# Four token blocks through the dense expert pass instead of three, with both expert tables split in two

## The chip, the cores and the metric

The kernel runs on one core of a Trainium2 chip. The metric is the device time of one execution in microseconds (us). Three runs of the kernel before gave a median of 3335.54 us (3333.65 to 3341.8).

## The reference

One decoder layer over 1024 tokens of width 1024, in float32. A token mixer (stick-breaking attention and an mLSTM) and a layer norm give `h`; what follows is a feed-forward layer of 16384 experts ("PEER"), of which each token uses 8 heads x 16:

```
s1, s2 = scores of h against two sets of 128 keys        # per head
idx, gates = top 16 of the 256 sums of the two top-16s   # expert = 128*i1 + i2
act = gelu(h . u_tab[idx])                               # 128 rows of 1024 per token
out = sum over the 128 chosen of gates * act * v_tab[idx]
h   = LN(alpha*h + out + sigmoid(h Wg) * (p Wp))
```

## The kernel before

Tokens are cut into 8 blocks of 128, which pass through the mixer in three groups, (0, 1), (2, 3, 4) and (5, 6, 7) (`BLOCKS`). Below, blocks are called by these numbers, 0 to 7. Per group `main()` issues: projections, then attention and mLSTM, then `branch` (gates, output projection, layer norm), `keys` (key scores and the top 16 of each half, on VectorE), then `choose` (top 16 of the sums, softmax; one block after the other, ending in the tile `vidx` of expert numbers) merged with `embed` (the `p Wp` part, tile `gs`) and the next group's projections.

The expert layer is done in two ways.

**Gathered** blocks (0, 1, 2, 5, 6): `Experts.first` fetches for each of the block's 128 choices one row of `u` per token by an indirect DMA on the GpSimd queue (line 1079, tile `vr`, six buffers) and VectorE multiplies and sums it (line 1099); `Experts.second` does the same with `v` (line 1111). Both are recorded by the helper in line 139. One such instruction with its DMA is called a row below: 256 rows a block, 512 KB each. A rate table places the rows between the other work, so each engine's order is fixed when the program is built; a layer norm ends each block.

**Dense** blocks (3, 4, 7, `DENSE`): `spread` (line 954) writes each block's gates as a matrix over all 16384 experts to DRAM (`Gd`): one-hot columns by VectorE and ScalarE (`ohA`, `ohB`, lines 977 to 985; the letters in `HOTS` say which engine does each of four), a product on TensorE (line 987), copies (line 989) and stores. `dense` (line 1009) then takes the experts in 128 steps of 128. A step loads 512 KB of `u` and 512 KB of `v`, splits `u` into a high and a low part of a shorter format (`split`, line 249: ScalarE copies, VectorE subtracts), scores with three products (line 273) of 384 columns for each of 8 slices, takes Gelu, multiplies by the gates (line 1043) and, one step later (`back`, line 1016), adds `y` times the unsplit float32 `v` into six PSUM banks for three blocks. Float32 products run in two passes. At the end `based` is added and a layer norm is taken.

The group that goes last issues in this order: split the dense blocks' inputs (`halve`), `keys`, `choose` of block 7 merged with `embed`, then `choose` of 5 and 6 merged with `dense`.

Of the kernel before, what the change touches and what calls it, by code (L numbers as in the profile page):

```python
# [18 lines left out]
D = 1024  # L19
S = 1024  # L20
P = 128
# [44 lines left out]
BLOCKS = [(0, 1), (2, 3, 4), (5, 6, 7)]  # L66
DENSE = (3, 4, 7)
OFF = (0, 256, 0)
# [4 lines left out]
SLOTS = 5  # L73
W = 384
# [45 lines left out]
def body(ctx: ExitStack, tc: tile.TileContext, a, out):  # L120
# [62 lines left out]
    def c6(name, shape=(P, 4, W), dt=F32):  # L183
        return sb.tile(list(shape), dt, name=name, tag="c6", bufs=8)

    def c4(name, shape=(P, D)):
        return sb.tile(list(shape), F32, name=name, tag="c4", bufs=NC4)

# [5 lines left out]

    def csel(name, shape=(P, 512)):
        return sb.tile(list(shape), F32, name=name, tag="cs", bufs=NCS)

# [55 lines left out]
    def load_piece(ap):  # L253
        wf = T([P] + list(ap.shape[1:]), F32, "wf", 8)
        dma.dma_start(wf, ap)
        return wf

    def split_piece(wf):
        if wf.shape[1] == 2:
            hl = [T([P, 2, 512], F32R, "wf", 8) for _ in range(2)]  # L260
            split(wf, *hl)
            return hl
        halves = []
        for i in range(2):
            halves.append([c2("hl", (P, 4, P), F32R) for _ in range(2)])
            split(wf[:, 4 * i:4 * i + 4, :], *halves[i])
        return halves
# [61 lines left out]
    def load_ln(i):  # L329
        r = []  # L330
        for n in "gb":
            src = a[f"ln{i}_{n}"]
            t = T([P, D], F32, f"ln2{n}") if i == 2 else c4(f"ln{n}_")
# [79 lines left out]
    ND = len(DENSE)  # L413
    Gd = dr.tile([ND, 8, 2, P, 64, 16], F32, name="Gd")

# [62 lines left out]
    def project(o):  # L478
# [25 lines left out]
        o.qT = c6("qT")  # L504
        o.vx = T([P, 3, NM, 129], F32, "vx", 1)
        vec.memset(o.vx[:, :, :, 128:129], 1.0)
# [447 lines left out]
    def spread(tb, vidx, gt):  # L954
# [7 lines left out]
        vec.tensor_copy(f, ii)  # L962
        by = HOTS
        pt = PT("z", (P, 4, P))
# [7 lines left out]
        for q in range(8):  # L972
# [19 lines left out]
            for i in range(2):  # L992
                dma.dma_start(Gd[d, q, i], st[i])

    def slot(tb):
        o = [o for o in blks if tb in o.tbs][0]
        j = tb - o.tbs[0]
        return o.h1T[:, :, j * P:(j + 1) * P]

    def halve():  # L1000

        r = [[c6("h1s", dt=F32R) for _ in range(2)] for _ in range(2)]
        for q in range(2):
            for d, tb in enumerate(DENSE):
                c = slice(d * P, (d + 1) * P)
                split(slot(tb)[:, 4 * q:4 * q + 4, :], *[t[:, :, c] for t in r[q]])
        return r

    def dense(h1s):

        w = ND * P
        acc = [[PT("g"), PT("g")], [PT("g"), PT("g")], [PT("z"), PT("z")]]
        gp = [[c6("gp", (P, 4 * ND, 8, 16)) for _ in range(2)] for _ in range(2)]
        todo = []

        def back(e, y, wv):
            for d in range(ND):
                for c in range(2):
                    pe.matmul(acc[d][c], y[:, d * P:(d + 1) * P], wv[:, c * 512:(c + 1) * 512],  # L1019
                              start=e == 0, stop=e == P - 1)  # L1020

        def load(e):
            if e < P:
                i, k = divmod(e, 64)
                src = Gd[:, :, i, :, k:k + 8, :].rearrange("d q p i t -> p (d q) i t")
                for c in range(2):
                    dma.dma_start(gp[e // 8 % 2][c], src[:, 4 * ND * c:4 * ND * (c + 1)])

        load(0)
        for e in range(P):  # L1030
            if e % 8 == 0:
                load(e + 8)
            wu = stream.get(experts[e][0])
            wv = stream.get(experts[e][1])[0]
            pu = PT("m")
            for k in range(8):
                i, j = divmod(k, 4)
                mm(pu[:, :w], [t[:, j, :] for t in wu[i]], [t[:, j, :] for t in h1s[i]], k == 0, k == 7)
            y = csel("y")[:, :w]
            act.activation(y, pu[:, :w], AF.Gelu)  # L1040
            y3 = y.rearrange("p (c a t) -> p c a t", c=2, t=16)
            for c in range(2):
                vec.tensor_tensor(y3[:, c], y3[:, c], gp[e // 8 % 2][c][:, :, e % 8, :], op=OP.mult)  # L1043
            todo.append((e, y, wv))
            if len(todo) > 1:
                back(*todo.pop(0))
            yield 9.2
        back(*todo.pop(0))
        g, b = ln2
        hs = []  # L1050
        for d, tb in enumerate(DENSE):
            h = c4("accd")
            dma.dma_start(h, based[tb * P:(tb + 1) * P, :])
            for c in range(2):
                cs = slice(c * 512, (c + 1) * 512)
                vec.tensor_tensor(h[:, cs], h[:, cs], acc[d][c], op=OP.add)
            hs.append(h)
        for d in layer_norm(hs, g, b):
            dma.dma_start(out[DENSE[d] * P:(DENSE[d] + 1) * P, :], hs[d])
            yield 1.0  # L1060


    class Experts:
# [41 lines left out]
        def second(self, tb, w, vidx, gt):  # L1105
            act.loose(w, w, AF.Gelu)
            vec.tensor_tensor(w, w, gt.rearrange("p h k -> p (h k)"), op=OP.mult)
            acc = r4("acc")
            dma.dma_start(acc, based[tb * P:(tb + 1) * P, :])
            for s in range(P):  # L1110
                self.row(vidx, s, (a["v"], lambda vr, s=s: evec.scalar_tensor_tensor(
                    acc, vr, w[:, s:s + 1], acc, op0=OP.mult, op1=OP.add)))
                yield ROW_US
            self.flush()
            g, b = ln2
# [22 lines left out]

    ln2 = []

    def main():
        yield from pre(blks[0])
        ln2.extend(load_ln(2))
        for i, o in enumerate(blks):
# [12 lines left out]
            else:  # L1157
                h1s = halve()
                yield from keys(o)
                ex.rate = RATES["last"]  # L1160
# [78 lines left out]
```

## Time and profile before

| what | value |
|---|---|
| median of three runs | 3335.54 us |
| the profiled execution, its own time | 3336.88 us |
| its span, first to last instruction | 3335.1 us |
| TensorE busy | 2974.0 us (89%) |
| VectorE busy | 2668.9 us (80%) |
| ScalarE busy | 1101.9 us (33%) |
| GpSimd busy | 1562.8 us (47%) |
| DMA, mean over the span | 310 GB/s |

Shares of busy time are averages over stages with different limits, so the stages are to be read one by one. Matmuls overlap in the records: the time that one costs is the distance from its start to the next start, and not its own length.

### The profile page before, as it was taken

The numbers are of one execution on the slowest core, as the hardware profiler recorded it, in microseconds if no ns is written. First come the engines' busy times: TensorE is split into PE (matmuls) and PEld (weight loads), VectorE is DVE, ScalarE is ACT, GpSimd is POOL, SyncE is SP. The second block draws the span as 40 slices with busy tenths as digits, with TensorE's granted clock in tenths as the row PEclk, the third lists the DMA queues.
The fourth block names the chain that finished last, engine by engine and source line by source line (L and its number), as shares of the span: only waits on it lengthen the run. The fifth ranks groups of instructions, "written<-read, shape, count | busy, mean of one in ns | idle before, by whom it ended". The sixth has DMA issues, their size and how long they took to land.

```text
span 3335.1 us, 38987 instructions
## 1 busy us (share of the span) xinstructions
PE 2974.0 (89%) x12105; PEld 1982.6 (59%) x12105; DVE 2668.9 (80%) x5661; ACT 1101.9 (33%) x2560; POOL 1562.8 (47%) x1313
## 2 busy tenths in 40 slices
PE   7997999969899837999898967899999999999990
PEld 6786654545464535556655545566666666666660
DVE  5635999788699999989887999967776777777788
ACT  4626234430611458556413145111111111111110
POOL 0000156557534553556665343644445555554565
PEclk9998998969999968999899989999999999999995
DMA  6444699989979989898799889999999999999997
GB/s 213 136 146 143 234 350 323 323 281 381 376 271 317 359 273 320 306 340 267 244 373 363 308 303 312 335 361 352 353 346 355 357 353 348 348 355 337 361 329 265
DMA packets 341825, 1035.22 MB, mean 310 GB/s; under 512 B 38512, under 2 KB 95216, under 8 KB 341616
## 3 DMA queue, kind: packets, MB, share of 16 engines
q0 software_dynamic: 184320, 671.17, 56.0%
q1 hardware_dynamic: 157296, 361.55, 30.3%
q8 instruction: 96, 1.57, 0.2%
q14 instruction: 113, 0.93, 0.1%
HBM read 991.17 MB, written 41.42 MB: 310 GB/s over the span
## 4 chain that ended last, share of the span: by engine, by line
PE 67%; DVE 16%; issue 8%; ACT 6%; DMA 2%; POOL 1%; SPq 0%; DVEq 0%; POOLq 0%; ACTq 0%
PE g L274 15%; PE g L1019 13%; PE z L1019 6%; PE m L278 5%; PE m L276 5%; PE m L277 5%; PE g L784 3%; DVE acc L139 3%; PE m L622 3%; ACT ohB L161 2%; PE z L583 2%; DVE vr L139 2%; PE g L276 2%; PE g L278 2%; PE g L277 2%
## 5 line engine op out<-in xcount | busy, mean ns | idle before, releaser
L1079 POOL DMA_INDIRECT vr<-in_u_dram,vidx x640 | 772.9, 1208 | 1013.1 <-DVE V L139 384.5
L1079 POOL DMA_INDIRECT vr<-in_v_dram,vidx x640 | 786.1, 1228 | 729.6 <-DVE acc L139 271.2
L139 DVE SCALAR_TENSOR_TENSOR acc<-vr,w,acc 128x1024 f32<-128x1024 f32 x640 | 817.9, 1278 | 43.6 <-DMA vr<-in_v_dram,vidx 34.4
L139 DVE SCALAR_TENSOR_TENSOR vr<-vr,h1r 128x1024 f32<-128x1024 f32 x640 | 780.0, 1219 | 55.8 <-DMA vr<-in_u_dram,vidx 40.9
L1019 PE MATMUL g<-wf,y 128*128 128x512 f32 x1024 | 462.8, 594 | 14.7 <-DVE y L1043 14.7
L161 ACT ACTIVATE hl<-wf 128x512 fp32r<-128x512 f32 x256 | 160.5, 628 | 765.7 <-PE m L278 599.5
L251 DVE TENSOR_TENSOR hl<-wf,hl 128x512 fp32r<-128x512 f32 x256 | 179.1, 701 | 292.8 <-PE m L277 244.7
L276 PE MATMUL m<-h1s,hl 128*128 128x384 f32 x1024 | 394.7, 385 | 3.5 <-ACT y L161 3.5
L278 PE MATMUL m<-h1s,hl 128*128 128x384 f32 x1024 | 347.8, 340 | 2.7 <-DVE hl L251 2.6
L274 PE MATMUL g<-hT,wf 128*128 128x384 f32 x1024 | 342.7, 489 | 5.8 <-DVE gs L851 3.2
L277 PE MATMUL m<-h1s,hl 128*128 128x384 f32 x1024 | 346.0, 338 | 0.0
L1019 PEld LDWEIGHTS g<-wf,y 128*128 128x128 f32 x1024 | 193.1, 190 | 201.9 <-issue 171.3
L274 PEld LDWEIGHTS g<-hT,wf 128*128 128x128 f32 x1024 | 191.7, 191 | 136.1 <-issue 7.7
L1019 PE MATMUL z<-wf,y 128*128 128x512 f32 x512 | 240.6, 592 | 0.0
L276 PEld LDWEIGHTS m<-h1s,hl 128*128 128x128 f32 x1024 | 194.1, 190 | 34.0 <-issue 29.4
L277 PEld LDWEIGHTS m<-h1s,hl 128*128 128x128 f32 x1024 | 194.1, 190 | 29.2 <-issue 29.2
L278 PEld LDWEIGHTS m<-h1s,hl 128*128 128x128 f32 x1024 | 193.8, 189 | 4.3 <-DVE hl L251 3.3
L987 PE MATMUL z<-ohA,ohB 128*128 128x128 f32 x768 | 137.9, 320 | 47.1 <-ACT ohB L161 18.7
L274 PE MATMUL g<-h1T,wf 128*128 128x384 f32 x512 | 173.1, 493 | 1.5 <-ACT h1T L161 1.4
L1019 PEld LDWEIGHTS z<-wf,y 128*128 128x128 f32 x512 | 97.3, 190 | 122.5 <-issue 122.2
L622 PE MATMUL m<-awT,vt 128*64 128x128 f32 x992 | 150.2, 303 | 18.6 <-ACT awT L173 10.4
L987 PEld LDWEIGHTS z<-ohA,ohB 128*128 128x128 f32 x768 | 112.1, 210 | 74.5 <-ACT ohB L161 53.1
(332 smaller groups left out, 4461.6 us busy)
## 6 DMA issues: line engine op xcount, KB each, us to landing
wf<-in_uE_dram SPq DMA_DIRECT2D x128, 512.0 KB
wf<-in_v_dram SPq DMA_DIRECT2D x128, 512.0 KB
wf<-in_wmain_dram SPq DMA_DIRECT2D x84, 512.0 KB
wf<-in_wgate_dram SPq DMA_DIRECT2D x48, 512.0 KB
wf<-in_wq_dram SPq DMA_DIRECT2D x48, 512.0 KB
Gd<-stage SPq DMA_DIRECT2D x48, 512.0 KB
gp<-Gd SPq DMA_DIRECT2D x32, 768.0 KB
wf<-in_wout_dram SPq DMA_DIRECT2D x24, 512.0 KB
```

Of the source, the lines that this page charges most:

```text
L139: x = getattr(vec, op)(*args, **kw)
L161: x = nc.scalar.activation(o, i, f, **kw)
L251: vec.tensor_tensor(lo, src, hi, op=OP.subtract)
L274: pe.matmul(o, l[0], r[0], start=first, stop=last)
L276: pe.matmul(o, l[0], r[0], start=first, stop=False)
L277: pe.matmul(o, l[0], r[1], start=False, stop=False)
L278: pe.matmul(o, l[1], r[0], start=False, stop=last)
L622: pe.matmul(po[rows, :P], vt[:, lo + s, row["e"] * 64:(row["e"] + 1) * 64], wT[:, s * P:(s + 1) * P], start=i == 0, stop=i == row["nb"] - 1)
L784: pe.matmul(acc, yT[k // 4][:, k % 4, n * P:(n + 1) * P], wo[u][k // 2][:, k % 2, :], start=k == 0, stop=k == 7)
L987: pe.matmul(pg[:, k], B[:, k], A[:, k], start=True, stop=True)
L1019: pe.matmul(acc[d][c], y[:, d * P:(d + 1) * P], wv[:, c * 512:(c + 1) * 512], start=e == 0, stop=e == P - 1)
L1079: pool.indirect_dma_start(out=vr, out_offset=None, in_=use[0], in_offset=bass.IndirectOffsetOnAxis(ap=idx[:, s:s + 1], axis=0))
```

## The change

Block 2 moves from the gathered blocks to the dense ones, so that 0, 1, 5 and 6 are gathered. In the dense pass `v` and `y` are split in two as `u` was, and the product with `v` becomes three products of the short format. Eight PSUM banks hold the sums of three blocks; the fourth block's product is taken for two steps at a time into a bank of the scoring pair (`pair`) and added up by VectorE in SBUF, in the place of block 5's `h1T`. `choose` of block 5 is issued ahead of the dense pass. `HOTS` for block 7 gives VectorE three of four one-hot columns. Gates are loaded for 6 steps at a time instead of 8. Pools change in size, and the last layer norm's vectors are loaded where they are used.

```
-DENSE = (3, 4, 7)
+DENSE = (7, 2, 3, 4)
+LAST = (5, 7)
+GE = 6
+NWF = 10
-HOTS = "DAAD"
+HOTS = {2: "DAAD", 3: "DAAD", 4: "DAAD", 7: "DDAD"}
...
     def split_piece(wf):
-        if wf.shape[1] == 2:
-            hl = [T([P, 2, 512], F32R, "wf", 8) for _ in range(2)]
+        if wf.shape[1] != 8:
+            hl = [T(list(wf.shape), F32R, "wf", NWF) for _ in range(2)]
...
-    stream.items += [(x, i == 0) for e in experts for i, x in enumerate(e)]
+    for e in range(P + 1):
+        stream.items += [(experts[e][0], True)] if e < P else []
+        stream.items += [(experts[e - 1][1], True)] if e else []
...
+        def score(e):
             wu = stream.get(experts[e][0])
-            wv = stream.get(experts[e][1])[0]
             pu = PT("m")
             for k in range(8):
                 i, j = divmod(k, 4)
-                mm(pu[:, :w], [t[:, j, :] for t in wu[i]], [t[:, j, :] for t in h1s[i]], k == 0, k == 7)
-            y = csel("y")[:, :w]
-            act.activation(y, pu[:, :w], AF.Gelu)
+                mm(pu, [t[:, j, :] for t in wu[i]], h1s[0][k], k == 0, k == 7)
+            y = csel("y")
+            act.activation(y, pu, AF.Gelu)
             y3 = y.rearrange("p (c a t) -> p c a t", c=2, t=16)
...
+            hl = c4("yhl", (P, 2, W4), F32R)
+            split(y, hl[:, 0], hl[:, 1])
+            ys[e] = hl
+
+        def part(o, e, d, c, first, last):
+            mm(o, [ys[e][:, i, d * P:(d + 1) * P] for i in range(2)],
+               [t[:, c * 512:(c + 1) * 512] for t in vs[e]], first, last)
+
+        def back(e):
+            vs[e] = stream.get(experts[e][1])
+            for d in range(n):
+                for c in range(2):
+                    part(acc[d][c], e, d, c, e == 0, e == P - 1)
+
+        def pair(e, c):
+            pg = PT("m")
+            part(pg, e, n, c, True, False)
+            part(pg, e + 1, n, c, False, True)
...
+                vec.tensor_tensor(s4, s4, p4, op=OP.add)
...
+        for e in range(P + 2):
+            if e % GE == 0:
+                load(e // GE + 1)
+            if e < P:
+                score(e)
+            if e % 2 and e > 1:
+                pair(e - 3, 1)
+            if 0 < e <= P:
+                back(e - 1)
+            if e % 2 == 0 and e:
+                pair(e - 2, 0)
...
-                yield from Merge(choose(o, [t for t in o.tbs if t in DENSE]), embed(o))
+                yield from Merge(choose(o, LAST), embed(o))
+                halve(h1s, [t for t in DENSE if t in o.tbs])
                 ex.rate = RATES["dense"]
-                yield from Merge(choose(o, [t for t in o.tbs if t not in DENSE]), dense(h1s))
+                yield from Merge(choose(o, [t for t in o.tbs if t not in LAST]), dense(h1s))
...
-    nc = bacc.Bacc("TRN2", target_bir_lowering=False, num_devices=1, dynamic_dma_scratch_size=8192)
+    nc = bacc.Bacc("TRN2", target_bir_lowering=False, num_devices=1, dynamic_dma_scratch_size=2048)
```

Three places show how the change moves instructions. Line numbers of the changed program stand a few higher (139 becomes 143, 276 to 278 become 280 to 282).

TensorE before, the end of a dense step: the last of 24 scoring products, the six float32 products of `back`, and the next step's scoring.

```order
L278 MATMUL m<-h1s,hl 128x384
L1019 MATMUL g<-wf,y 128x512 x4
L1019 MATMUL z<-wf,y 128x512 x2
L276 MATMUL m<-h1s,hl 128x384
L277 MATMUL m<-h1s,hl 128x384
```

TensorE now, the end of a scoring (`h1l` is the last low part of the inputs), two products of `back`, then the first three of a `pair`.

```order
L281 MATMUL m<-h1l,hl 128x512
L282 MATMUL m<-h1s,hl 128x512
L280 MATMUL g<-wf,yhl 128x512
L281 MATMUL g<-wf,yhl 128x512
L280 MATMUL m<-wf,yhl 128x512
L281 MATMUL m<-wf,yhl 128x512
L282 MATMUL m<-wf,yhl 128x512
```

A step has 24 scoring products of 512 columns, and 18 in `back` and on average 6 in `pair` (768 in all), in place of 24 of 384 columns and 6 in float32.

VectorE before, where block 2's `vidx` is ready: block 3's choice goes on behind it (`top`, `pos` and `cv` are its tiles).

```order
L139 SCALAR_TENSOR_TENSOR acc<-vr,w,acc 128x1024
L139 CAST vidx<-idf 128x128
L139 MAX top<-cv 128x8
L139 MAX_INDEX pos<-top,cv 128x8
```

VectorE now, at the same place.

```order
L143 CAST vidx<-idf 128x128
L143 SCALAR_TENSOR_TENSOR vr,w<-vr,h1r 128x1024
L966 TENSOR_SCALAR seli<-vidx 128x128
L967 TENSOR_SCALAR seli<-vidx 128x128
L143 SCALAR_TENSOR_TENSOR acc<-vr,w,acc 128x1024
L968 CAST self<-seli 128x256
```

Block 2's spread now stands between its `vidx` and the rest of block 3's choice, with rows of the gathered blocks among it.

VectorE before, in `keys` of the last group (`sc` holds scores, `V` and `I` the best values and places).

```order
L804 MAX V<-sc 128x8 x3
L807 MAX V<-sc 128x8 x3
L139 SCALAR_TENSOR_TENSOR acc<-vr,w,acc 128x1024
L805 MAX_INDEX I<-V,sc 128x8 x3
L808 MAX_INDEX I<-V,sc 128x8 x3
```

VectorE now, the same place.

```order
L810 MAX V<-sc 128x8 x3
L811 MAX_INDEX I<-V,sc 128x8 x3
L812 MATCH_REPLACE sc<-V,sc 128x128 x3
L813 MAX V<-sc 128x8 x3
L814 MAX_INDEX I<-V,sc 128x8 x3
```

No row stands in `keys` any more. Counted over VectorE's order, 736 rows stood ahead of the first dense gate product and 544 behind it; now 535 and 489.

## Rows read from the trace of the kernel before

**Rows 1.** The page, part 1: busy time by engine.
```profile
PE 2974.0 (89%) x12105; PEld 1982.6 (59%) x12105; DVE 2668.9 (80%) x5661; ACT 1101.9 (33%) x2560; POOL 1562.8 (47%) x1313
```

**Rows 2.** Busy time by stage: stretch, us, five engines, granted clock, DMA share, GB/s.
```profile
1015.00:1300.00 285.00, 206.45 (x860) 136.07 (x858) 277.22 (x762) 145.46 (x418) 134.75 (x108) 0.88 0.89 313
1300.00:1791.00 491.00, 448.72 (x1844) 274.00 (x1843) 420.45 (x637) 238.91 (x532) 293.33 (x239) 0.92 0.88 316
1791.00:1914.00 123.00, 123.00 (x432) 73.48 (x431) 116.87 (x413) 17.58 (x38) 51.20 (x52) 0.99 0.88 314
1914.00:2058.00 144.00, 105.53 (x468) 77.06 (x467) 139.77 (x405) 80.75 (x222) 54.73 (x49) 0.88 0.90 306
2058.00:3242.00 1184.00, 1166.13 (x4472) 802.05 (x4473) 873.93 (x1434) 206.60 (x376) 623.92 (x491) 0.99 0.96 348
```

**Rows 3.** TensorE in order of time, one dense step: start, length, line, operation.
```profile
2604.15 3.59 PE L1019 MATMUL g<-wf,y 128*128 128x512 f32 x8
...
2609.65 0.33 PE L278 MATMUL m<-h1s,hl 128*128 128x384 f32 x1
...
2613.29 0.34 PE L278 MATMUL m<-h1s,hl 128*128 128x384 f32 x1
2613.47 3.59 PE L1019 MATMUL g<-wf,y 128*128 128x512 f32 x8
```

**Rows 4.** TensorE in order of time, group one: ten split products of 512 columns.
```profile
131.21 0.39 PE L277 MATMUL g<-wf,vr 128*128 128x512 f32 x1
...
133.50 0.62 PE L276 MATMUL g<-wf,vr 128*128 128x512 f32 x2
```

**Rows 5.** VectorE instructions by line and form: busy us, mean ns, idle before.
```profile
L139 DVE SCALAR_TENSOR_TENSOR acc<-vr,w,acc 128x1024 f32<-128x1024 f32 x640 | 817.9, 1278 | 43.6 <-DMA vr<-in_v_dram,vidx 34.4 <-DMA acc<-based 1.1 <-DVE vr L139 0.9
L139 DVE SCALAR_TENSOR_TENSOR vr<-vr,h1r 128x1024 f32<-128x1024 f32 x640 | 780.0, 1219 | 55.8 <-DMA vr<-in_u_dram,vidx 40.9 <-issue 5.8 <-DVE vr L139 0.8
L251 DVE TENSOR_TENSOR hl<-wf,hl 128x512 fp32r<-128x512 f32 x256 | 179.1, 701 | 292.8 <-PE m L277 244.7 <-issue 39.8 <-PE m L278 4.1
L251 DVE TENSOR_TENSOR wf<-wf 128x1024 fp32r<-128x1024 f32 x68 | 83.0, 1221 | 73.9 <-ACT wf L161 71.8 <-PE g L784 2.1
L1043 DVE TENSOR_TENSOR y<-y,gp 128x192 f32<-128x192 f32 x256 | 80.4, 351 | 4.3 <-DMA gp<-Gd 4.3
L977 DVE TENSOR_TENSOR ohA<-iota,sel 128x512 f32<-128x512 f32 x96 | 65.4, 681 | 0.0
L985 DVE TENSOR_SCALAR ohB<-iota,sel 128x128 f32<-128x128 f32 x192 | 57.5, 339 | 0.0
```

**Rows 6.** VectorE in order of time: `vidx` of blocks 2, 3, 4 and 7.
```profile
1069.44 0.23 DVE L139 CAST vidx<-idf 128x128 uint32<-128x128 f32 x1
...
1105.61 0.21 DVE L139 CAST vidx<-idf 128x128 uint32<-128x128 f32 x1
...
1234.76 0.21 DVE L139 CAST vidx<-idf 128x128 uint32<-128x128 f32 x1
...
1972.04 0.22 DVE L139 CAST vidx<-idf 128x128 uint32<-128x128 f32 x1
```

**Rows 7.** TensorE's waits at 1015 to 1300 us (first row) and 1300 to 1791 us.
```profile
PE z L965 <- DVE rs L376: 40.4, 1, 40.4
...
PE m L394 <- ACT mx L161: 10.1, 1, 10.1
PE m L622 <- ACT awT L173: 6.7, 5, 2.9
```

**Rows 8.** The end, in order of time: TensorE's last products, and VectorE behind them.
```profile
3246.04 1.88 PE L1019 MATMUL z<-wf,y 128*128 128x512 f32 x4
...
3249.56 1.28 DVE L1056 TENSOR_TENSOR accd<-accd,z 128x512 f32<-128x512 f32 x2
3250.76 10.52 DVE L139 SCALAR_TENSOR_TENSOR acc<-vr,w,acc 128x1024 f32<-128x1024 f32 x8
...
3312.76 1.29 DVE L370 BATCH_NORM_STATS2 st<-acc 128x6 f32<-128x512 f32 x2
```

More of the change, by code (lines that the diff above doesn't have):

```diff
@@ L72 @@
 FASTQ = {0}
-SLOTS = 5
+SLOTS = 6
 W = 384
@@ L193, in c2, with csel @@
         return sb.tile(list(shape), dt, name=name, tag="c2", bufs=NC2)
-    def csel(name, shape=(P, 512)):
-        return sb.tile(list(shape), F32, name=name, tag="cs", bufs=NCS)
+    def csel(name, shape=(P, 512), dt=F32):
+        return sb.tile(list(shape), dt, name=name, tag="cs", bufs=NCS)
     first = [c4("xt") for _ in BLOCKS[0]]
@@ L253, in load_piece @@
     def load_piece(ap):
-        wf = T([P] + list(ap.shape[1:]), F32, "wf", 8)
+        wf = T([P] + list(ap.shape[1:]), F32, "wf", NWF)
         dma.dma_start(wf, ap)
@@ L332, in load_ln @@
             src = a[f"ln{i}_{n}"]
-            t = T([P, D], F32, f"ln2{n}") if i == 2 else c4(f"ln{n}_")
+            t = T([P, D], F32, "vr", K) if i == 2 else c4(f"ln{n}_")
             dma.dma_start(t, bass.AP(tensor=src.tensor, offset=src.offset, ap=[[0, P], [1, D]]))
@@ L992, in spread @@
             for i in range(2):
[L993 to L1007, printed above, removed]
+                dma.dma_start(Gd[d, q, :, i * 64:(i + 1) * 64], st[i])
@@ new lines, in body, with halve, parts @@
+    W4 = ND * P
+    def halve(h1s, tbs):
+        for tb in tbs:
+            c = slice(DENSE.index(tb) * P, (DENSE.index(tb) + 1) * P)
+            for k, n, hi, lo in h1s[1]:
+                split(h1Ts[:, k:k + n, DCOL + c.start:DCOL + c.stop], hi[:, :, c], lo[:, :, c])
+    def parts():
+        t = [c6("h1s", (P, 3, W4), F32R) for _ in range(5)]
+        rest = csel("h1l", dt=F32R)[:, None, :]
+        runs = [(0, 3, t[0], t[3]), (3, 3, t[1], t[4]), (6, 1, t[2][:, 0:1, :], t[2][:, 2:3, :]),
+                (7, 1, t[2][:, 1:2, :], rest)]
+        return [(hi[:, i, :], lo[:, i, :]) for k, n, hi, lo in runs for i in range(n)], runs
@@ L1009, in dense @@
     def dense(h1s):
-        w = ND * P
+        n = ND - 1
         acc = [[PT("g"), PT("g")], [PT("g"), PT("g")], [PT("z"), PT("z")]]
[L1013 to L1017, printed above, removed]
-                for c in range(2):
[L1019 to L1032, printed above, removed]
+        sums = h1Ts[:, :, 0:P]
+        gp = {}
+        ys, vs, pend = {}, {}, []
+        def load(g):
+            if g * GE < P:
+                m = min(GE, P - g * GE)
+                gp[g] = [c6("gp", (P, 4 * ND, GE, 16)) for _ in range(2)]
+                src = Gd[:, :, :, g * GE:g * GE + m, :].rearrange("d q p i t -> p (d q) i t")
+                for c in range(2):
+                    dma.dma_start(gp[g][c][:, :, :m, :], src[:, 4 * ND * c:4 * ND * (c + 1)])
@@ L1055, in dense @@
                 cs = slice(c * 512, (c + 1) * 512)
-                vec.tensor_tensor(h[:, cs], h[:, cs], acc[d][c], op=OP.add)
+                if d < n:
+                    vec.tensor_tensor(h[:, cs], h[:, cs], acc[d][c], op=OP.add)
+                else:
+                    hv = h[:, cs].rearrange("p (k t) -> p k t", k=4)
+                    vec.tensor_tensor(hv, hv, sums[:, 4 * c:4 * c + 4, :], op=OP.add)
             hs.append(h)
-        for d in layer_norm(hs, g, b):
-            dma.dma_start(out[DENSE[d] * P:(DENSE[d] + 1) * P, :], hs[d])
-            yield 1.0
+        for i in range(0, ND, 2):
+            for d in layer_norm(hs[i:i + 2], g, b):
+                dma.dma_start(out[DENSE[i + d] * P:(DENSE[i + d] + 1) * P, :], hs[i + d])
+                yield 1.0
     class Experts:
@@ L1157, in main @@
             else:
-                h1s = halve()
                 yield from keys(o)
+                h1s = parts()
+                halve(h1s, [t for t in DENSE if t not in o.tbs])
                 ex.rate = RATES["last"]
-                yield from Merge(choose(o, [t for t in o.tbs if t in DENSE]), embed(o))
+                yield from Merge(choose(o, LAST), embed(o))
+                halve(h1s, [t for t in DENSE if t in o.tbs])
                 ex.rate = RATES["dense"]
-                yield from Merge(choose(o, [t for t in o.tbs if t not in DENSE]), dense(h1s))
+                yield from Merge(choose(o, [t for t in o.tbs if t not in LAST]), dense(h1s))
     now = bg = 0.0
```

37 lines of the change are left out of this document (20 added, 17 removed).

## The prediction

> **What bounds the kernel now.** I read the page's busy shares first: TensorE 89%, VectorE 80% [rows 1], which says only that two engines compete. The table of stages then says where each of them decides. From 2058 to 3242 us, the dense pass, TensorE is busy 1166 of 1184 us at a granted clock of 0.99 (2.4 GHz), VectorE 874 [rows 2]: this stage belongs to TensorE. From 1015 to 1300 us (choices and spreads of the second group) VectorE is busy 277 of 285 us and TensorE only 206; TensorE waits once for 40.4 us at line 965, where a spread begins [rows 2, 7]. The list puts that wait down to a small norm instruction (`rs`), but line 965 transposes what is made from `vidx`, and what is late is VectorE's queue as a whole. From 1300 to 1791 us (mixer of the last group) TensorE is busy 449 of 491 us; from 1791 to 1914 us (`keys`) 123 of 123. From 1914 to 2058 us (choice and spread of block 7) VectorE is full again, 140 of 144 us [rows 2].
>
> The step of the dense pass is read off the order of time: the float32 products begin at 2604.15 and again at 2613.47 us, so a step takes 9.32 us [rows 3]. Inside it, 21 starts of 384-column products lie between 2609.65 and 2613.29 us, 0.173 us each (3.64 / 21). The 24 of them make 4.16 us, so the 12 passes of the six float32 products cost 5.16 us, 0.43 each.
>
> At the end TensorE stops at 3247.9 us, and the span goes on for 87 us: VectorE still has rows of the last gathered block up to 3312.8 us, and then four layer norms, 22 us [rows 8]. So the gathered work is late by about 65 us beyond the dense pass, and no more.
>
> **The change, part by part.** The sum is made against the profiled execution, 3336.9 us (span 3335.1), which is 1.3 us above the median and inside its scatter. A measurement of this kernel can tell about 0.3%, 10 us, from no change.
>
> *A dense step.* 24 products of 384 columns and six in float32 go; 48 split products of 512 columns come (24 to score, 18 in `back`, 6 on average in `pair`). Their price is in the trace, in group one: ten starts from 131.21 to 133.50 us, 0.229 us each [rows 4], the same rate per column as the 0.173 of today's 384 columns. 48 x 0.229 = 10.99 us instead of 9.32. Over 128 steps: 1407 - 1193 = **+214 us**. TensorE is the limit there, so all of it lies on the path. The splitting of `v` trades 5.16 us of float32 for 18 x 0.229 = 4.12 us, which is a gain; the fourth block is what costs: 6 x 0.229 = 1.37 us in the second product and 24 x 0.056 = 1.34 us in scoring.
>
> *What VectorE must carry in a step.* 489 rows over the 122 steps that have any, 4.0 a step at 1.25 us (mean of 1278 and 1219 ns): 5.0 us. Splits of `u`, 2 x 0.70; of `v`, 1.22; of `y`, 0.70 like the 512-wide `hl`; gate products, between 2 x 0.35 (as now) and 2 x 0.47 (by size), I take 0.85; the addition of a `pair`, 0.64 like the final one from PSUM (1.28 for two) [rows 5, 8]. Sum 9.8 us of 10.99, 89%, against 74% now. TensorE covers that, and I cost it at nothing; between the end of a scoring and the `back` that uses it lie the previous `back` and the next scoring, some 9.6 us, for a Gelu, two products and a split. If the cover is gone, a step lasts as long as VectorE's.
>
> *The spread of block 2, at 1015 to 1300 us.* Its work on VectorE is 32 x 0.681 + 64 x 0.339 = 43.5 us [rows 5]: a lower bound, since VectorE is full there. The upper bound: block 3's choice, without a spread beside it, took from 1069.44 to 1105.61 us, 36.2 us; block 4's, beside the spread of block 3, took 129.2 us [rows 6]; that is 93 us more, rows included. In VectorE's order 28 more rows now stand ahead of the third `vidx`, 28 x 1.28 = 36 us. 43.5 + 36 = **+80 us**, near the upper end. The attention of the last group stands behind the third spread in TensorE's queue, so it starts that much later.
>
> *Fewer rows at 1300 to 1914 us.* Ahead of the first dense gate product 201 rows fewer stand in VectorE's queue, nearly all of them missing here. That is over 200 us of VectorE, but TensorE decides: its waits from 1300 to 1791 us add up to 42 us in 24 entries, of which the first two are shown [rows 7]; a mean clock of 0.92 means that 16% of the stretch, 79 us, ran at 1.2 GHz, of which at most half, 39 us, could come back. So between 0 and -81 us; I take two thirds, **-54 us**, since most of those waits end on ScalarE and VectorE work that will be earlier. In `keys` TensorE never waits, so 52 rows fewer there bring 0 (bound -20).
>
> *From `keys` to the first `back`.* Between the first `gs` and block 7's `vidx` 18 rows go (-23 us) and the choice of block 5 comes in, between 17 and 36 us from the 36.2 above, without or with the rows in it; I take 26: **+3 us**. Block 7's spread gives VectorE 32 more one-hot columns, 32 x 0.339 = 11 us, and takes work off ScalarE; between 0 and +11, **+6 us**. The dense pass thus starts 80 - 54 + 3 + 6 = **35 us later** (bounds -64 and +117).
>
> *The end.* All rows now stand ahead of the last steps, and only the four norms are left: 22 us as now, eight additions at 0.64 us, and about 2 us for two of the four `accd` loads, whose buffers are held by `y` until TensorE is done: 29 us instead of 87, **-58 us** (22 to 39 us as ends).
>
> *Other queues.* GpSimd issues 256 row DMAs fewer. SP issues some 30 loads and stores more (gates and norm vectors), but its weight loads stand about two steps ahead of their use, so neither queue lies on the path. DMA carries 4.0 x 0.52 + 1.05 + 0.26 = 3.4 MB per 10.99 us, 310 GB/s, under the 348 of now [rows 2].
>
> **Sum:** 3336.9 + 214 + 35 - 58 = **3528 us**, 5.8% slower.
>
> **The rivals.**
>
> *VectorE takes over the dense pass* (3614 us). Before, splits of `u` sat idle for TensorE for 245 us, 1.9 us a step [rows 5]: the queue is in order, and what stands behind such a wait stands too. Should 1.9 us of it remain beside 9.8 us of work, a step takes 11.7 us, 0.7 x 122 = 86 us more. Against it: those waits are what a queue with spare time shows, and they shrink when it is late. Chance 0.08.
>
> *The products run at the floor of the clock* (3432 us). 512 columns at 2.4 GHz are 213 ns; 48 x 0.213 = 10.24 us, 96 us less over the pass. Against it: neither 384 nor 512 columns did so in these rows, 0.173 against a floor of 0.160. Chance 0.04. The Trainium skill, page "TensorE: Matmul & The Clock Gate", section "Wait — 56ns, not 53.3ns?", gives 215.7 ns start to start for 512 columns at the full clock, which would make a step 10.35 us and the time 3446 us; this case's trace does not agree, with 229 ns.
>
> *VectorE was the limit all along, and the dense pass starts early* (3322 us, faster). 201 rows less are 251 us, and the spread, the choice of block 5 and the extra columns give 80 back. Were VectorE's queue all that decides from 1015 to 2058 us, the pass would start 171 us earlier instead of 35 later, and the kernel would gain 0.4%. The two cross where the start moves by -156 us. For it: VectorE is nearly full in that whole stretch. Against it: TensorE's idle time there is 79 + 42 + 0 + 38 = 159 us [rows 2], and the first and last parts are just where VectorE gets more to do. Chance 0.05.
>
> *The terms cancel* (about 3337 us): an early start by some 150 us and nothing else. Chance 0.02.
>
> **How the numbers follow.** The forecast's own case has 0.81: 3528 us. Its unknown ends together are 3337 + 214 - 64 - 65 = 3422 and 3337 + 214 + 117 - 48 = 3620 us; they will not all fall on one side, so the range takes 3440 to 3605, which holds the floor-rate case nearly and most of the VectorE case short of its price. Slower by over 0.3%: 0.81 + 0.08 + 0.04 = 0.93; within: 0.02; faster: 0.05.
>
> **What would show it.** In the profile after: split products of 512 columns at 0.229 us and dense steps of about 11.0 us at full clock, 1407 us in all; VectorE near 89% there; a third spread between 1015 and 1400 us, and attention after it some 80 us late; the first `back` near 2095 us; about 29 us after TensorE's last product. Wrong would be: steps above 11.3 us with TensorE waiting for `yhl` or `hl`, a dense pass that starts before 2000 us, or rows left behind the last step.

## The result and the profile after

The changed kernel takes 3559.64 us (median of four runs, 3555.77 to 3565.23), against 3338.49 us for the kernel before (3333.65 to 3341.8). The ratio is 1.0665, with a 95% interval from 1.0643 to 1.0687: slower by 6.65%, or 221 us. 3528 was predicted, so the forecast is 32 us short. The profiled execution took 3565.23 us, 5.6 above the median of its runs.

The page, part 1, of the changed kernel, beside [rows 1]:

```profile
PE 3243.5 (91%) x13900; PEld 2342.5 (66%) x13900; DVE 2722.2 (76%) x5803; ACT 1358.7 (38%) x2948; POOL 1282.1 (36%) x1057
```

TensorE has 270 us more to do, VectorE 53 more, although 256 of its 1280 rows are gone: the splits of `v` and `y`, the spread of block 2 and the sums of the pairs took their place.

Busy time by stage of the changed kernel, with the columns of [rows 2]. The stretches are the same stages, at their new times, with edges rounded by eye:

```profile
1015.00:1385.00 370.00, 250.18 (x1119) 170.29 (x1117) 358.75 (x898) 204.01 (x610) 173.56 (x146) 0.86 0.90 316
1385.00:1855.00 470.00, 444.42 (x1829) 268.56 (x1829) 231.61 (x351) 229.76 (x518) 85.32 (x67) 0.94 0.41 143
1855.00:1978.00 123.00, 119.36 (x418) 72.23 (x419) 57.08 (x375) 23.04 (x55) 0.00 (x0) 0.97 0.26 84
1978.00:2130.00 152.00, 97.51 (x443) 70.60 (x441) 140.73 (x555) 68.26 (x161) 31.25 (x30) 0.83 0.68 220
2130.00:3540.00 1410.00, 1409.30 (x6072) 1141.48 (x6072) 1157.19 (x1667) 420.57 (x629) 641.01 (x482) 1.00 0.86 298
```

Three things stand out. The first stretch is 85 us longer (78 by the first attention product, 1306.8 and 1385.0 us), and VectorE is as full there as before. In the second VectorE is busy 232 of 470 us instead of 420 of 491, and TensorE does not hurry because of it: most of the 21 us between these two stretches is rounding of their edges, and from the first attention product to the last output product it is 466.4 us before and 464.6 now. In the last TensorE never pauses: 1409 of 1410 us.

One dense step, TensorE in order of time, beside [rows 3]:

```profile
2699.02 0.39 PE L280 MATMUL m<-h1s,hl 128*128 128x512 f32 x1
...
2704.32 0.39 PE L282 MATMUL m<-h1s,hl 128*128 128x512 f32 x1
2704.55 0.40 PE L280 MATMUL m<-wf,yhl 128*128 128x512 f32 x1
...
2710.14 0.39 PE L280 MATMUL m<-h1s,hl 128*128 128x512 f32 x1
...
2721.26 0.39 PE L280 MATMUL m<-h1s,hl 128*128 128x512 f32 x1
```

From one step to the next are 11.12 us, for 48 products: 0.2317 us each.

VectorE's `vidx` of blocks 2, 3, 4 and 7, beside [rows 6]:

```profile
1068.89 0.23 DVE L143 CAST vidx<-idf 128x128 uint32<-128x128 f32 x1
...
1208.64 0.21 DVE L143 CAST vidx<-idf 128x128 uint32<-128x128 f32 x1
...
1313.27 0.21 DVE L143 CAST vidx<-idf 128x128 uint32<-128x128 f32 x1
...
2036.15 0.22 DVE L143 CAST vidx<-idf 128x128 uint32<-128x128 f32 x1
```

TensorE's waits at 1015 to 1385 us, beside the first of [rows 7]:

```profile
PE z L971 <- DVE self L968: 76.7, 3, 39.6
```

The first product of `back` in TensorE's order, in the kernel before and in the changed one:

```profile
2043.80 1.88 PE L1019 MATMUL g<-wf,y 128*128 128x512 f32 x4
```

```profile
2130.70 0.80 PE L280 MATMUL g<-wf,yhl 128*128 128x512 f32 x1 [21.80 <-ACT yhl L165]
```

The end of the dense pass in the changed kernel, and VectorE's last four normalizing products, beside [rows 8]:

```profile
3539.79 0.40 PE L282 MATMUL m<-wf,yhl 128*128 128x512 f32 x1
```

```profile
3553.91 2.48 DVE L391 SCALAR_TENSOR_TENSOR accd<-accd,rs,vr 128x1024 f32<-128x1024 f32 x2
...
3556.90 2.48 DVE L391 SCALAR_TENSOR_TENSOR accd<-accd,rs,vr 128x1024 f32<-128x1024 f32 x2
```

The sum by these marks: the first `back` moved from 2043.8 to 2130.7 us (+87), the pass from there to TensorE's last product went from 1204 to 1409.5 us (+205), and what follows it from 87 to 23 us (-64). 3335.1 + 87 + 205 - 64 = 3563, the span of 3563.5. (In the kernel before, 2058 us, where the stage of the dense pass was cut, is the second `back` and not the first.)

These marks carry some scatter: the profiled execution is the slowest of its four, and in two runs below whose edits lie inside the pass the first attention product came at 1379.5 us instead of 1385.0 and the first `back` at 2119.4 instead of 2130.7.

### The profile page after: what moved, and what is told of

It reads as the page before. It is cut to its first block, busy times and chain, and to the rows that moved or that the text cites. A ratio compares the mean times of both kernels' runs of the same rounds, so it can differ in the third digit from the quotient of the medians.

```text
span 3563.5 us, 42592 instructions
## 1 busy us (share of the span) xinstructions
PE 3243.5 (91%) x13900; PEld 2342.5 (66%) x13900; DVE 2722.2 (76%) x5803; ACT 1358.7 (38%) x2948; POOL 1282.1 (36%) x1057
## 4 chain that ended last, share of the span: by engine, by line
PE 76%; DVE 11%; ACT 7%; issue 4%; DMA 1%; POOL 0%; SPq 0%; DVEq 0%; ACTq 0%; POOLq 0%
PE g L278 18%; PE m L281 8%; PE m L280 8%; PE m L282 8%; PE g L280 5%; PE g L281 5%; PE g L282 5%; PE m L628 3%; PE g L790 3%; ACT ohB L165 2%; PE z L589 2%; PE z L281 2%; PE z L280 2%; PE z L282 2%; DVE vr L143 1%
## 5 line engine op out<-in xcount | busy, mean ns | idle before, releaser
L1122 POOL DMA_INDIRECT vr<-in_u_dram,vidx x512 | 624.2, 1219 | 1504.6 <-DVE top L143 489.0
L1122 POOL DMA_INDIRECT vr<-in_v_dram,vidx x512 | 654.1, 1277 | 655.2 <-DVE acc L143 418.7
L143 DVE SCALAR_TENSOR_TENSOR acc<-vr,w,acc 128x1024 f32<-128x1024 f32 x512 | 655.1, 1279 | 25.8 <-DMA vr<-in_v_dram,vidx 21.0
L143 DVE SCALAR_TENSOR_TENSOR vr<-vr,h1r 128x1024 f32<-128x1024 f32 x512 | 623.6, 1218 | 24.9 <-DMA vr<-in_u_dram,vidx 18.6
L280 PE MATMUL m<-h1s,hl 128*128 128x512 f32 x1024 | 402.8, 393 | 6.6 <-ACT h1p L177 4.0
L282 PE MATMUL m<-h1s,hl 128*128 128x512 f32 x1024 | 403.2, 394 | 0.0
L281 PE MATMUL m<-h1s,hl 128*128 128x512 f32 x896 | 354.8, 396 | 0.0
L255 DVE TENSOR_TENSOR wf<-wf 128x1024 fp32r<-128x1024 f32 x196 | 239.2, 1220 | 75.6 <-ACT wf L165 70.0
L165 ACT ACTIVATE wf<-wf 128x1024 fp32r<-128x1024 f32 x196 | 207.3, 1059 | 164.6 <-DVE wf L255 73.9
L165 ACT ACTIVATE y<-m 128x512 f32<-128x512 f32 x128 | 76.7, 600 | 441.5 <-PE m L282 441.5
L280 PE MATMUL g<-wf,yhl 128*128 128x512 f32 x512 | 202.6, 397 | 21.8 <-ACT yhl L165 21.8
L993 PE MATMUL z<-ohA,ohB 128*128 128x128 f32 x1024 | 174.2, 313 | 50.1 <-ACT ohB L165 19.9
L281 PE MATMUL g<-wf,yhl 128*128 128x512 f32 x512 | 202.7, 396 | 0.0
L282 PE MATMUL g<-wf,yhl 128*128 128x512 f32 x512 | 201.3, 395 | 0.0
```

Of the source, the lines that this page charges most:

```text
L143: x = getattr(vec, op)(*args, **kw)
L165: x = nc.scalar.activation(o, i, f, **kw)
L255: vec.tensor_tensor(lo, src, hi, op=OP.subtract)
L280: pe.matmul(o, l[0], r[0], start=first, stop=False)
L281: pe.matmul(o, l[0], r[1], start=False, stop=False)
L282: pe.matmul(o, l[1], r[0], start=False, stop=last)
```

## The experiments

Two questions were put to the chip: whether TensorE alone sets the dense pass, and what sets the 1100 us ahead of it, where the prediction's start of the pass was off. Unless something else is said, an edit is made to the changed kernel, and times are compared with its 3559.6 us. Of the kernel before, each group of runs gave a median of 3336.6 to 3338.8 us.

### The dense pass without the fourth block's product

```
-            if e % 2 and e > 1:
-                pair(e - 3, 1)
...
-            if e % 2 == 0 and e:
-                pair(e - 2, 0)
```

> The changed kernel without the fourth block's second product: its six TensorE products a step, the addition in SBUF and the sums are left out (that block's part of the output is missing). Theory (a dense step costs its TensorE products at 0.229 us each and nothing else): a step falls from 10.99 to 42 x 0.229 = 9.62 us, the pass by 128 x 1.37 = 176 us, the time from about 3560 to 3385 us. Rival (VectorE sets the pace): VectorE still has about 9.2 us a step, so steps would stay above 10.3 us and the time above 3475 us.

Measured: 3481.5 us (one run): the theory's steps, and a time that only the rival allowed, for a reason that neither names. The steps became what 42 products make, from 2701.40 to 2711.12 and 2720.84 us, 9.72 each (42 x 0.2314), and TensorE ended at about 3332 us. But the kernel did not end there:

Busy time by stage of this run:

```profile
2130.00:3330.00 1200.00, 1200.00 (x5186) 973.15 (x5185) 961.26 (x1398) 411.21 (x615) 509.33 (x404) 1.00 0.89 311
3340.00:3455.00 115.00, 0.00 (x0) 0.00 (x0) 99.31 (x82) 0.00 (x0) 81.21 (x70) 0.50 0.93 341
```

TensorE was busy without a gap and still decided the pass; rows of the gathered blocks then lay bare, with DMA at 0.93, up to 3451.5 us. The step is as priced. What was missed is the next bound: the rows fill the longer pass and not the shorter one. Whether VectorE (busy 99 of 115 us there) or the DMA that feeds it (VectorE waits for it 14 us) paces these last rows was not separated.

### Three dense blocks, with both tables split

```
-DENSE = (7, 2, 3, 4)
+DENSE = (7, 3, 4)
```

Block 2 is gathered again and `pair` falls away; with them the early choice of block 5, the one-hot columns of block 7, the scoring of 384 columns, the 8 steps of gates and the grouping of the last norms go back to what they were. The splits of `v` and `y`, the order in which weights are loaded and the sizes of the pools stay changed.

> The changed kernel with block 2 gathered again, so that only the second product's split is left of the change (three dense blocks, scoring 384 columns wide, no sums in SBUF). TensorE has 24 x 0.173 + 18 x 0.229 = 8.3 us a step in place of 9.32. Theory (the 544 rows behind the start of the dense pass, at 1.25 us of VectorE each beside some 4 us of VectorE a step, then decide): TensorE is done some 100 us earlier or waits, the rows are later still behind it, and the time stays within 3300 to 3370 us. Rival (the dense pass alone decides): 128 x 1.03 = 132 us come off, 3205 us.

Measured: 3396.3 us (3394.0 to 3402.5), 1.0178 of the kernel before (1.0161 to 1.0195). The range of the theory was missed by 26 us, and the rival's gain is nowhere.

Busy time by stage of this run:

```profile
2058.00:3135.00 1077.00, 1052.94 (x5236) 950.37 (x5235) 924.15 (x1531) 391.47 (x625) 481.80 (x386) 0.99 0.92 331
3135.00:3375.00 240.00, 1.01 (x5) 0.48 (x3) 210.02 (x201) 0.31 (x1) 172.52 (x149) 0.51 0.95 349
```

A step fell from 9.32 to 8.38 us (starts at 2603.72, 2612.10 and 2620.48), and TensorE was done at 3136 us, 112 earlier than in the kernel before. VectorE, which has 1.22 us more per step for the split of `v` and 0.55 for that of `y`, ended its rows at 3370 us instead of 3312. So the split, with what stays beside it, is a gain for TensorE and a loss of 1.8% for the kernel, since the kernel before is held by its rows as much as by TensorE.

### VectorE's sums left out, and read three times

In the first of the two kernels only the first and the last pair of steps reach SBUF; in the second, two copies stand beside each addition.

```
-            if e == 0:
+            if e in (0, P - 2):
                 vec.tensor_copy(s4, p4)
-            else:
-                vec.tensor_tensor(s4, s4, p4, op=OP.add)
```

```
                 vec.tensor_tensor(s4, s4, p4, op=OP.add)
+                for _ in range(2):
+                    vec.tensor_copy(c2("twice", (P, 4, P)), p4)
```

> The changed kernel without VectorE's additions for the fourth block: of the 64 pairs of steps only the first and the last are copied out of PSUM, so 124 additions of 0.64 us (79 us of VectorE) are missing, and the fourth block's output is incomplete. TensorE's products are all there. Theory (TensorE's 48 products set the step, VectorE has 9.0 us of work in 11.0): steps stay at 11.0 us, the dense pass at 1405 to 1412, kernel 3550 to 3565 us. Rival (VectorE's queue decides in the pass, its sums being the last straw): steps 10.4 us, kernel 3480 to 3500.

> The changed kernel with VectorE's reading of the fourth block's PSUM tile done three times over: beside each addition two copies of the same tile into scratch, 256 more instructions of about 0.6 us, some 155 us of VectorE, 1.2 us a step. Theory (VectorE's 9.0 us a step become 10.3, still under 11.0): kernel 3555 to 3580 us. Rival (no room left beside rows, splits and gates): the pass lengthens by most of it, kernel 3660 to 3720.

Measured: 3551.6 us (3549.0 to 3557.5) without the sums, 3583.8 us (3581.0 to 3586.2) with three readings.

Busy time of the dense pass, of the kernel without sums:

```profile
2119.00:3528.00 1409.00, 1408.52 (x6072) 1141.45 (x6072) 1086.86 (x1543) 415.91 (x629) 649.65 (x482) 1.00 0.86 298
```

and of the kernel with three readings, with TensorE's waits behind its first `back`:

```profile
2119.00:3556.00 1437.00, 1415.59 (x6072) 1138.75 (x6072) 1294.92 (x1911) 419.59 (x629) 612.47 (x482) 1.00 0.84 293
```

```profile
PE m L280 <- ACT y L165: 20.8, 33, 0.7
PE m L280 <- DVE twice L1071: 0.3, 1, 0.3
```

With 70 us taken from VectorE the pass is 1409 us as before; what this kernel is faster by came ahead of it (first `back` at 2119.5 us, and at 2119.3 in the other). With the two copies, which raise VectorE's busy time from 1157 to 1295 us, the pass is 28 us longer, a fifth of the 138 us, and TensorE begins to wait, 33 times, for the bank that the Gelu empties late; the time is 4 us above the theory's range. So the sums cost nothing, and VectorE is not the bound of the pass. Its room is real but small, and gives out gradually: at 82% busy TensorE never waits, at 90% it begins to.

### Two edits that did not move what they should

```
-            ex.rate = RATES["mix"]
+            ex.rate = RATES["mix"] if i < 2 else 0.0
```

the same for `branch` and `keys`, in the kernel before; and `RATES["choose"]` set to 0 for the second group in the changed kernel.

> The kernel before with no gathered rows issued from the last group's mixer to its key scores (about 1300 to 1914 us); they come later, so the end will be later and is not what is asked. Theory (TensorE and ScalarE set that stretch, VectorE does not): from the first attention product at 1306.8 us to the first gs at 1914.6 us, 608 us now, at most 20 us are saved, as the changed kernel showed with 593. Rival (VectorE's rows do hold it back, as the prediction took for two thirds of the waits): 54 us or more are saved, 554 or less.

> The changed kernel with no rows issued during the choices and spreads of blocks 2 to 4; they move behind. Theory (VectorE's queue sets that stretch, and 118 rows at 1.28 us, 151 us, ride in it): the third vidx moves from 1313 to about 1180 us, the first attention product from 1385 to about 1255 us, the mixer stretch keeps its length although it now carries the rows, and the time falls by 100 to 135 us to 3425 to 3460 us. Rival 1 (the spread's chain through ScalarE and TensorE, some 71 us each, sets it): only 40 to 70 us come off. Rival 2 (rows given to the mixer lengthen it by what they take): the time stays at about 3560 us.

Measured: 3446.1 us (one run) and 3550.4 us (3548.7 to 3554.6). Neither tests its theory. The rates bound how many rows are offered, but the rows in hand are placed all the same: counted in VectorE's trace, the mixer kept its rows in the first kernel (124 of `u` and 104 of `v`, as before), the second group's choices theirs in the second (36 and 62 instead of 36 and 63; third `vidx` at 1305.9 us, where the runs with edits inside the pass alone have 1307.6). The 9 us that the second took less are thus read as scatter, and so are the 8 us of the kernel without sums.

What the first one shows is another stretch, from the last output product to the first `back`, in the kernel before and in this run:

```profile
1773.20:2043.80 270.60, 222.26 (x869) 145.63 (x867) 253.05 (x770) 110.54 (x292) 107.98 (x103) 0.91 0.89 316
```

```profile
1775.00:2005.80 230.80, 210.56 (x866) 136.94 (x865) 142.43 (x694) 107.26 (x290) 0.00 (x0) 0.98 0.38 139
```

With 97 rows of `v` fewer there it is 40 us shorter. The dense pass began and ended earlier (TensorE's end at 3187 us instead of 3248), and the rows still to do, 97 more than before, ran on to 3422 us.

### Rows stopped by a real wait

Rows are counted, stopped at 290 from the second group's mixer to the last group's, and let go by the expert list of block 4, so that none stand in VectorE's program between the second group's first gates and its third `vidx`.

```
+            if tb == 4:
+                evec.gate = x
...
+            ex.cap = 290 if i == 1 else 1 << 30
...
+            if ex.n >= ex.cap:
+                bg = now
+                break
```

> The changed kernel, its rows of the gathered blocks stopped at 290 until the spread of the fourth block is done (by a real wait on that block's list of experts, so that no row stands in VectorE's program between the first gates of the second group and its third list). 207 first and 79 second halves of rows leave that stretch and go into the mixer's stretch behind it. Theory (VectorE with its rows in program order sets 1015 to 1385, the mixer's stretch has half of VectorE to spare): third list from 1313 to 1200 to 1230 us, first attention product from 1385 to 1270 to 1300, mixer's stretch 465 to 490 us although it now carries some 230 halves of rows, whole kernel 3450 to 3490 us against 3560. Rival 1 (the chain of the spread on ScalarE sets the stretch, rows fill its gaps): third list 1290 to 1313, kernel 3540 to 3565. Rival 2 (the rows in the mixer's stretch lengthen it by what the spread's stretch gains): first attention product about 1290, first back product again about 2130, kernel about 3560.

Measured: 3503.9 us (3495.3 to 3507.1), 56 less than the changed kernel: 14 us above the theory's range and well under the first rival's. Busy time of this run between its three lists of block 2, 3 and 4:

```profile
1027.10:1170.90 143.80, 126.86 (x555) 81.91 (x553) 63.38 (x226) 72.82 (x212) 0.00 (x0) 0.95 0.41 141
1170.90:1249.90 79.00, 48.89 (x259) 37.00 (x259) 58.49 (x217) 61.58 (x195) 0.00 (x0) 0.87 0.27 107
```

and of the changed kernel between the same three:

```profile
1068.90:1208.60 139.70, 99.21 (x443) 66.52 (x441) 131.79 (x310) 68.74 (x206) 75.38 (x63) 0.87 0.95 360
1208.60:1313.30 104.70, 50.99 (x259) 40.39 (x259) 103.90 (x280) 64.66 (x198) 45.46 (x36) 0.74 0.83 280
```

VectorE went from 132 to 63 us of work in the first interval, and the interval did not shrink (143.8 us). TensorE is busy 127 of 144 us there and waits for nothing, and VectorE's one-hot columns wait for TensorE's products of the spread (line 995 in this run), between which the next group's projections stand (192 products of them in this interval, 136 in the changed kernel):

```profile
DVE ohB L993 <- PE z L995: 68.7, 14, 7.2
```

In the second interval 26 us were won, and 42 ahead of the first list. So a part of this stretch is VectorE's queue with rows in it, and for a part TensorE's queue is nearly as long, which a full VectorE hides from the reader.

### The fourth block's choice and spread beside the key scores

```
-ORDER = [(0, 1), (2, 3, 4)]
+ORDER = [(0, 1), (2, 3)]
...
-                yield from keys(o)
+                yield from Merge(keys(o), choose(blks[1], (4,)))
```

Two small tiles (`V` and `I`) get a fourth buffer for it.

> The changed kernel with choice and spread of the fourth block alone moved from the second group's stretch into the stretch of the key scores of the last group; the dense tables and steps stay. Theory (the added spread costs 78 us only because TensorE has nothing to do beside it): first attention product from 1385 to about 1300 us as in the kernel before, the stretch of the key scores 123 us becomes 125 to 165, first back product from 2130 to 2055 to 2095, kernel 3485 to 3525 us. Rival (VectorE has the same work in all and sets the time from 1015 to 2130 as a whole): first back product 2120 to 2140, kernel about 3560.

Measured: 3480.3 us (3479.4 to 3482.8), 79 less, and 5 us under the theory's range. The first attention product came at 1275.7 us instead of 1385.0 (109 earlier), and from the last product of line 790 to the first `back` passed 306 us instead of 281. The same choice and spread of one block thus cost 109 us in one place and 25 in the other, where TensorE and VectorE have each other's work beside them.

### Both, and the same stop in the kernel before

In the changed kernel both edits together, with the stop released by block 3's list, since block 4's now comes later:

```
-            if tb == 4:
+            if tb == 3:
                 evec.gate = x
```

> Both of the two edits: rows stopped at 290 until the third block's list is done, and the fourth block's choice and spread beside the last group's key scores. Theory: the two gains add up, first attention product at 1190 to 1230 us, first back product at 1980 to 2030, kernel 3400 to 3460 us. Rival (rows moved behind the spread lengthen the stretches after it): first back product 2060 to 2100, kernel 3480 to 3520, as with the later spread alone. In neither case below the kernel before, since the dense steps of 11 us stay: 128 of them are 1410 us against 1189.

Measured: 3449.8 us (3447.1 to 3454.9), 110 less than the changed kernel, within the theory's range, as is the first `back` at 2016.1 us, though the two gains of 56 and 79 do not quite add up. It is the best of the versions tried with four dense blocks, and still 1.0337 of the kernel before (1.0319 to 1.0354).

In the kernel before the stop alone, with its edit as above (`tb == 4`):

> The kernel before with the same stop of the rows at 290 until the fourth block's list is done. It has 640 second halves of rows against 512 and no slack at its end. Theory (rows of VectorE and DMA bound the kernel before as much as TensorE does): first attention product from 1307 to 1200 to 1240 us and the dense pass ends 40 to 80 us earlier than 3248, but the rows that were put off come out behind it, and the kernel takes 3320 to 3400 us. Rival (TensorE alone bounds it and what TensorE starts earlier is gained in full): 3260 to 3290 us.

Measured: 3459.8 us (3452.5 to 3462.8), 1.036 of the kernel before: the theory's direction, 60 us beyond its range. TensorE's attention began at 1254.0 us instead of 1306.8 and its pass ended at 3224.6 instead of 3247.9; 97 rows of `v` more stood behind the first `back`, and the rows ran on to 3436 us. An earlier start of TensorE is no gain in a kernel whose rows end last; the run of the kernel before with rows put off, above, shows the same. This one does not weigh the stop alone, as the next table shows.

### One number for the mixer, from six kernels

From the first product of the last group's attention (line 583, or 589 after the change) to the first of its output projection (784 or 790), us:

| kernel | from, to | length | TensorE busy | VectorE busy | ScalarE busy | clock | DMA |
|---|---|---|---|---|---|---|---|
| before | 1306.8, 1726.2 | 419.4 | 395 | 367 | 204 | 0.93 | 0.87 |
| changed | 1385.0, 1801.7 | 416.7 | 396 | 229 | 203 | 0.93 | 0.42 |
| rows stopped | 1319.4, 1747.1 | 427.7 | 404 | 368 | 207 | 0.91 | 0.83 |
| block 4 late | 1275.7, 1691.5 | 415.8 | 396 | 284 | 207 | 0.93 | 0.55 |
| both | 1238.7, 1663.6 | 424.9 | 400 | 374 | 210 | 0.92 | 0.83 |
| before, rows stopped | 1254.0, 1703.7 | 449.7 | 408 | 372 | 263 | 0.90 | 0.81 |

VectorE's work varies by 145 us and the length between the first five by 12. TensorE's 395 us are a floor under it. The last one is 30 us longer at the same load of VectorE, and its trace shows another difference: ScalarE loads a table for its functions 49 times there instead of 4 times. The largest group of these loads:

```profile
L161 ACT ACT_TABLE_LOAD x43 | 55.2, 1283 | 0.8
```

They are nearly all of ScalarE's 59 us more. That they are the cause of the 30 us was not shown by a run without them.

## Why the prediction came out as it did

The size of the result lay within the range, and the main mechanism was right: TensorE pays for the fourth block in a dense pass that it bounds alone. One term was wrong in size and in its ground. Term by term, by the profiled executions:

| term | predicted | measured |
|---|---|---|
| dense pass, from the first `back` to TensorE's last product | +214 | +205 |
| spread of block 2, to the first attention product | +80 | +78 |
| mixer, to its last output product | -54 | -2 |
| `keys`, choice and spread of block 7, to the first `back` | +9 | +11 |
| end | -58 | -64 |
| sum | +191 | +228 |

The prediction had the start of the pass 35 us later, "near 2095 us", counted from the stage's edge at 2058 us. The first `back` of the kernel before is at 2043.8 us, so the start is 87 us later, and the 52 us between are the mixer's term.

**The mis-sized term is "Fewer rows at 1300 to 1914 us", -54 us.** It took two thirds of what 42 us of waits and 39 us of lower clock would allow, on the ground that "most of those waits end on ScalarE and VectorE work that will be earlier". The prediction's own [rows 2] had TensorE busy 449 of 491 us. Between the two products of the table above only 24 us of TensorE were idle, and 21 are now. These waits end mostly on short chains between TensorE and ScalarE or VectorE, for example, at 1385 to 1855 us:

```profile
PE m L628 <- ACT awT L177: 9.1, 5, 2.7
PE z L589 <- DMA kt<-kTd: 6.8, 1, 6.8
PE z L589 <- DVE art L605: 5.0, 3, 3.8
```

Those of the kernel before are in [rows 7]. They did not shrink with the rows gone: five waits for `awT` made 6.7 us before and make 9.1 now. That each lasts as long as the other engine needs for its own piece is a reading; no run tests one by itself. Nor did the clock come back: 0.93 in both. The prediction should have taken its upper bound, 0, from the stage's owner. With 0 in place of -54 it gives 3582 us, and the differences of the other terms, -9 for the pass, -6 for the end, -2 each for the spread and the mixer and +2 for what lies between the mixer and the first `back`, bring that to 3565, as the profiled execution has it. That the forecast is off by less than its worst term is because these smaller errors lay the other way.

The other half of that term, `keys`, was put at 0 since TensorE never waits there. The kernel before with rows put off says that the rows did count behind the mixer: 97 fewer made the way from the last output product to the first `back` 40 us shorter. In the changed kernel the choice of block 5 and the additional columns stand in that place; what each costs there was not measured apart.

**The dense pass** was priced by a row from another part of the kernel, 0.229 us; the pass itself shows 0.2317, which is 16 us over 128 steps. It came out near all the same, in part by luck. In the pass before TensorE waited 20 us, most of it near its start, which 128 steps of 9.32 us leave out:

```profile
PE g L1019 <- DVE y L1043: 14.7, 2, 13.5
```

In the changed one it waits for nothing behind its first `back`. And three of the 128 scorings lie ahead of the first `back` in both kernels, which takes 4 us more off the new pass, with its dearer scorings. That the sums of the pairs cost nothing was right and is shown by leaving them out. VectorE has 1157 us of work in 1410, 9.0 us a step, against 9.8 predicted; the gate products at 0.42 us and the additions at 0.68 are near what was taken.

**The spread of block 2** came out at +78 us for +80, but not quite as argued. It was summed as work on a full VectorE, 43.5 us and 36 of rows, and VectorE is full there (132 of 140 us between the lists of blocks 2 and 3). The runs show what the sum does not hold: with no rows in VectorE's queue this interval is as long as with them, since TensorE has 127 of 144 us to do in it. Taking the rows out brings 66 us in the stretch as a whole (first attention product at 1319.4 instead of 1385.0), moving one choice and spread elsewhere 109. That a sum over VectorE alone came within 2 us of a stretch in which two queues are nearly as long is in part luck.

**The end**: 23 us instead of 29. The additions for two of the four blocks were done from 3535.6 to 3539.2 us, while TensorE took its last products; the 29 us had set them behind it.

**The rivals.** That VectorE takes over the pass did not happen: TensorE waited for nothing in it. It is near, though, as the two copies more show. The products did not run at the floor of the clock: 0.2317 us for 512 columns at a granted clock of 1.00 is above the 0.213 of that rival. The Trainium skill, page "TensorE: Matmul & The Clock Gate", section "Wait — 56ns, not 53.3ns?", has 215.7 ns there; this trace does not agree, with 231.7 for its split products. The early start that was the rival on the fast side needed -156 us and got +87. Relieving VectorE brings next to none of it in the mixer, as the mixer's table shows, and 40 us behind it, as the kernel before with rows put off shows.

No version tried beat the kernel before. TensorE's busy time in the changed kernel, 3243.5 us, is only 92 under the whole span of the kernel before, and the best version has it busy 3215.9 of 3448.4 us.

## What to carry to other kernels

Before crediting an engine's relief to a stage, ask who owns the stage: in this mixer TensorE was busy 94% of the time, the rest was mostly short waits, and 138 us less of VectorE returned 3 us. Where two resources are nearly balanced, as TensorE and the rows are in the kernel before, taking work from one and giving it to the other is priced as two kernels: each run with three dense blocks that ended TensorE's pass sooner ended its rows later, and the kernel with them. And a full engine in a stretch does not prove that it sets it, when a scheduler pours deferrable work into every gap; taking that work out by a real dependence tells, where changing a rate did not.

## What was not expected of the hardware

TensorE's granted clock in the mixer did not come back when the other engines fell quiet. Between 1600 and 1700 us of the changed kernel DMA moves 1 GB/s, GpSimd nothing, VectorE is under half busy, and TensorE, busy 92 of 100 us, has a mean granted clock of 0.86, so some 28% of these 100 us at 1.2 GHz and the rest at 2.4:

```profile
1600.00:1700.00 100.00, 91.67 (x472) 62.79 (x471) 44.85 (x83) 63.75 (x152) 0.00 (x0) 0.86 0.00 1
```

In the dense pass, with DMA at 298 GB/s and VectorE at 82%, it is 1.00, but for the start: behind 22 us of waiting, its first products come 0.427 us apart (ten starts below, 2131.29 to 2135.56 us), at a granted clock of 0.50 (1.2 GHz), and from 2136.3 us on 0.23 us apart, at 1.00 (2.4 GHz):

```profile
2131.29 0.63 PE L281 MATMUL g<-wf,yhl 128*128 128x512 f32 x1
...
2135.56 0.63 PE L281 MATMUL z<-wf,yhl 128*128 128x512 f32 x1
```

And the start-to-start time of a split product of 512 columns is not quite the same everywhere at full clock: 0.229 us in group one [rows 4], 0.2317 in the pass, where the steps from 2209.74 to 3510.78 us are all 11.12 us long. Inside the step shown above the 24 scoring products take 5.53 us, 0.2304 each, and the 24 others 5.59 us, 0.2329 each. The cause is open.
